# Attention in a diffusion backbone: value matmuls gathered into groups, score products between transposes, TensorE's order fixed by hand

## Chip, cores and metric

One core of a Trainium2 chip runs the whole program: two layers of a diffusion backbone over 1024 latent tokens and 256 context tokens, in fp32. The metric is the device time of one execution in microseconds (us), as the median of several runs. Lower is better.

## What is computed

Each layer normalises its input, projects it once into the inputs of four head groups, runs the groups, gates their outputs and projects back. The change concerns the two attention groups alone. Cut to what matters:

```python
def attend_dense(q, k, v):                      # latent attention: 4 heads, 1024 + 256 keys
    s = jnp.einsum('bqhd,bkhd->bhqk', q, k).astype(jnp.float32) * (q.shape[-1] ** -0.5)
    p = jax.nn.softmax(s, axis=-1).astype(v.dtype)
    return jnp.einsum('bhqk,bkhd->bqhd', p, v)
...
    def row_fn(args):                           # neighbourhood attention: a window of 8 x 16 plus 256 context keys
        ...
        s_loc = jnp.einsum('bjmhd,bijnhd->bhjmin', q_r, k_blk).astype(jnp.float32) * scale + b_r[None]
        s_ctx = jnp.einsum('bjmhd,bchd->bhjmc', q_r, kc).astype(jnp.float32) * scale
        s = jnp.concatenate([s_loc.reshape(*s_loc.shape[:4], nloc), s_ctx], axis=-1)
        p = jax.nn.softmax(s, axis=-1).astype(v.dtype)
        ...
        return (jnp.einsum('bhjmin,bijnhd->bjmhd', p_loc, v_blk)
                + jnp.einsum('bhjmc,bchd->bjmhd', p_ctx, vc))
```

In the first layer the context tokens also attend to themselves.

## The kernel before

A layer is a list of stages: projections, then latent attention, then neighbourhood attention together with the first blocks of the output projection, then the rest of the output projection. The attention stages are cut into **units**, kept in the list `units`:

- `Mla`, a *full unit*: 256 latent queries of two heads against all 1280 keys. Eight per layer, four for each pair of heads. In the first layer each pair also has a *small unit*, the 256 context queries against the context keys alone, which stands ahead of the pair's four full ones.
- `NaCtx`: the context's own queries in neighbourhood attention, two units, first layer only.
- `Na`: a block of 128 queries of two heads against 384 local and 256 context keys. Sixteen per layer: the eight of the first half of the rows (`half` 0), then the eight of the second half.

Work on a unit has four parts. `prep` makes the queries (`Mla`) or loads the bias table (`Na`). *Score products* (`scores`) write a PSUM bank of tag `psb` (five of them). VectorE takes their maximum, and ScalarE the exponential into SBUF: this is the softmax of the unit, and its row sums come with it. *Transposes* (`transpose(n)`) turn 128 x 128 pieces of the exponentials into a bank of tag `pst` (two of them), four pieces at a time, and `evac` copies the bank to a tile of tag `pt`, on ScalarE and VectorE in turn. *Value matmuls* (`values(n)`) multiply a `pt` tile by the values into the one bank `psv`. They use 64 columns of the array for each head, so the two heads write the two halves of the bank's partitions, while all other matmuls of the attention use 128 columns. An fp32 matmul runs as two instructions, a transpose as one. At the end `normalise` divides by the row sums, through two or four more transposes of line L716.

The loop at the end of `layer` goes through the units. While unit u runs its `steps`, the *pieces* of unit u+1 (its score products) are written between them, and `units[u+2].prep()` behind step `PREP` = 2. In `Mla.steps`, step k is the transposes of key block k+1 and then the value matmuls of block k, so transposes run one block ahead of values. There are ten key blocks in a full unit; a piece is the whole score work of one head and one half of the queries (three products and the softmax), and four pieces go behind steps 0, 2, 4 and 6 (`PIECES`). In `Na` the three steps are: transposes 0 and 1; values 0 and transposes 2; values 1 and 2. Its one piece is all the scores of the next unit.

This written order is not the order of the program. The kernel is built with a scheduler (`TileContext(nc, schedule_with_timeline_sim=True)`) that places each engine's instructions by its own estimate of when they are ready, within the dependencies of the tiles and their buffers, so on every engine it may pull work forward. Behind each of the last eight `Na` units the loop also writes one block of the output projection, `out_block(fb, [k0])`: 24 matmuls of 512 columns over the first 512 tokens, whose inputs (`merged(0)`) are ready when the first half has been normalised. The scheduler can use these as filler.

## Time and profile before

| | |
|---|---|
| median of 3 runs | 1508.65 us (1508.60 to 1509.43) |
| profiled execution, span from first to last instruction | 1511.4 us |
| TensorE busy in it | 1464.8 us, 97% |
| VectorE, ScalarE, GpSimd busy | 51%, 38%, 31% |
| latent attention, first and second layer | about 466 to 642 and 1165 to 1335 us from the span's start |
| neighbourhood attention, first and second layer | about 642 to 743 and 1335 to 1440 us |

The profile shows one execution, 2.7 us longer than the median of the runs. PE is TensorE, PEld its weight loads (they overlap the matmuls), DVE is VectorE, ACT ScalarE, POOL GpSimd, SP the engine that issues most DMAs. The end of a matmul in the profile is modelled, and matmuls overlap in the pipeline, so a busy PE can still lose time: the distance from one start to the next tells what a matmul costs. PEclk is the share of TensorE's full clock (2.4 GHz) that was granted; 0.50 is the lower level, 1.2 GHz.

### The profile page before, as it was taken

Reading aid. Unit: us, or ns where it says so; the run is one execution under the profiler, and the core shown is the slowest. Engines: PE = TensorE matmul, PEld = TensorE weight load, DVE = VectorE, ACT = ScalarE, POOL = GpSimd, SP = SyncE. Lnnn points to the kernel's source line nnn. Section 1 sums busy time; section 2 is a strip of 40 time slices with the busy share of each in tenths; the row PEclk is TensorE's granted clock in tenths of the full one; section 3 lists DMA queues with packets and bytes.
Section 4 is the critical chain, followed back from the end, with each engine's and each line's share of the span. In section 5 each row is a group of like instructions: output and inputs, shape, how many; then the busy total and the mean of one; then the engine's idle time right before and its main releaser. Section 6 shows DMA issues by size and latency. Waiting matters only on the chain.

```text
span 1511.4 us, 23233 instructions
## 1 busy us (share of the span) xinstructions
PE 1464.8 (97%) x8964; PEld 1176.5 (78%) x8964; DVE 772.2 (51%) x1873; ACT 575.9 (38%) x1303; POOL 464.8 (31%) x369
## 2 busy tenths in 40 slices
PE   4999999999999999999999999999999999999996
PEld 3788888988887667677788988898887776667786
DVE  5878657063026767654465752201213676754373
ACT  5511111122226656554343421112223666654442
POOL 2235334041220110535623253412231010253741
PEclk8999999999999999999999999999999999999998
DMA  9412335355450222654433101123472041663241
GB/s 355 171 58 98 112 100 169 102 178 181 140 105 1 57 57 85 129 155 116 147 123 123 42 28 43 48 89 121 155 255 38 15 83 37 155 159 98 77 149 56
DMA packets 80943, 166.46 MB, mean 110 GB/s; under 512 B 8129, under 2 KB 34753, under 8 KB 80705
## 3 DMA queue, kind: packets, MB, share of 16 engines
q1 hardware_dynamic: 63808, 136.66, 27.1%
q0 software_dynamic: 15936, 27.27, 8.9%
q8 instruction: 70, 1.15, 0.3%
q10 hardware_dynamic: 1088, 1.05, 0.2%
q14 instruction: 41, 0.33, 0.1%
HBM read 135.33 MB, written 33.82 MB: 112 GB/s over the span
## 4 chain that ended last, share of the span: by engine, by line
PE 86%; DVE 5%; POOL 3%; issue 3%; DMA 2%; ACT 1%; SPq 0%; DVEq 0%; POOLq 0%; ACTq 0%
PE psb L159 63%; PE psv L832 6%; PE pst L822 6%; PE psv L957 3%; PE pst L944 3%; PE psb L917 1%; PE psb L924 1%; POOL s L184 1%; DVE s L186 1%; DVE g L466 1%; PE pst L716 1%; POOL g L1064 1%; POOL wl L323 1%; DMA wr<-in_wtb 0%; PE pst L270 0%
## 5 line engine op out<-in xcount | busy, mean ns | idle before, releaser
L159 PE MATMUL psb<-g,wh 128*128 128x512 f32 (+1 forms) x2400 | 695.0, 374 | 0.9 <-ACT g L374 0.8
L159 PEld LDWEIGHTS psb<-g,wh 128*128 128x128 f32 x2400 | 433.4, 190 | 84.6 <-issue 2.6
L159 PE MATMUL psb<-g,wl 128*128 128x512 f32 (+1 forms) x1200 | 446.4, 373 | 0.4 <-DVE wl L323 0.4
L159 PEld LDWEIGHTS psb<-g,wl 128*128 128x128 f32 x1200 | 227.4, 189 | 42.1 <-issue 2.2
L323 POOL TENSOR_TENSOR wl<-wr,wh 128x1024 fp32r<-128x1024 f32 (+2 forms) x64 | 150.1, 2348 | 304.6 <-ACT wh L318 303.8
L701 DVE COPY pt<-pst 128x512 f32<-128x512 f32 x132 | 86.7, 657 | 119.4 <-PE pst L822 51.3
L159 PE MATMUL psb<-g,st 128*128 128x512 f32 (+1 forms) x600 | 143.0, 371 | 3.5 <-ACT wl L811 2.2
L799 DVE TENSOR_REDUCE s<-psb 128x1 f32<-128x512 f32 (+1 forms) x200 | 113.8, 588 | 39.7 <-PE psb L159 39.3
L318 ACT CAST wh<-wr 128x1024 fp32r<-128x1024 f32 (+2 forms) x56 | 56.1, 1007 | 161.6 <-PE psb L159 126.7
L159 PEld LDWEIGHTS psb<-g,st 128*128 128x128 f32 x600 | 95.6, 191 | 18.3 <-ACT wl L811 2.8
L703 ACT COPY pt<-pst 128x512 f32<-128x512 f32 (+1 forms) x132 | 73.7, 558 | 92.9 <-PE pst L822 45.6
L832 PE MATMUL psv<-pt,g 128*64 128x256 f32 x656 | 101.7, 401 | 0.4 <-DVE x L722 0.4
L298 DVE CUSTOM_DVE_ANT_0 tmp<-g,x 128x512 f32<-128x512 f32 x112 | 92.9, 882 | 10.0 <-POOL x L431 7.2
L184 POOL TENSOR_TENSOR s<-s,mhalf 128x4 f32<-128x4 f32 (+3 forms) x35 | 36.7, 1048 | 146.9 <-DVE s L240 56.2
L159 PE MATMUL psb<-g,g 128*128 128x256 f32 (+1 forms) x576 | 76.8, 289 | 0.0
L159 PEld LDWEIGHTS psb<-g,g 128*128 128x128 f32 x576 | 71.7, 191 | 0.8
L320 POOL TENSOR_SCALAR wh<-wr 128x1024 fp32r<-128x1024 f32 x16 | 44.3, 2772 | 78.1 <-PE psb L159 40.5
L159 PE MATMUL psb<-st,g 128*128 128x288 f32 (+1 forms) x456 | 64.3, 289 | 0.0
L832 PEld LDWEIGHTS psv<-pt,g 128*64 128x64 f32 x656 | 34.6, 135 | 37.2 <-issue 20.4
L811 ACT ACTIVATE g<-psb,s,rq 128x512 f32<-128x512 f32 x64 | 49.3, 776 | 34.2 <-DVE s L806 31.7
L822 PEld LDWEIGHTS pst<-ident,g 128*128 128x128 f32 x256 | 26.7, 140 | 45.1 <-issue 43.5
L159 PEld LDWEIGHTS psb<-st,g 128*128 128x128 f32 x456 | 60.4, 188 | 0.5 <-issue 0.2
(205 smaller groups left out, 2074.8 us busy)
## 6 DMA issues: line engine op xcount, KB each, us to landing
g<-in_wmod SPq DMA_DIRECT2D x48, 512.0 KB, 4.7
wr<-in_wtb SPq DMA_DIRECT2D x46, 512.0 KB, 3.8
wr<-in_wout SPq DMA_DIRECT2D x27, 512.0 KB, 4.3
st<-in_nab SPq DMA_DIRECT2D x24, 384.0 KB, 3.3
x<-in_xT SPq DMA_DIRECT2D x32, 256.0 KB, 4.4
g<-scr_q POOLq DMA_DIRECT2D x32, 256.0 KB, 5.1
x<-x SPq DMA_DIRECT2D x24, 256.0 KB, 3.1
g<-scr_k POOLq DMA_DIRECT2D x20, 256.0 KB, 4.5
```

What stands on the lines that cost most here:

```text
L159: m = pe.matmul(out, l_, r_, start=(i == 0), stop=(i == n - 1))
L184: pool.tensor_tensor(r0, v, mhalf[:, :n], ALU.pow)
L298: dve.tensor_tensor_reduce(junk, w[:, hf * 512:hf * 512 + 512], crow[cond, hf], 1.0, 0.0, ALU.mult, ALU.add, part[:, i, cond, hf:hf + 1])
L318: act.copy(hi, raw)
L323: (pool if lo_eng == "pool" else dve).tensor_tensor(lo, raw, f(hi), ALU.subtract)
L701: dve.tensor_copy(dst, src)
L703: act.copy(dst, src)
L799: dve.reduce_max(mx[:, i:i + 1], s_, AX.X)
L811: act.activation(dst, sps[i], AF.Exp, bias=nb[:, 1:2], scale=rq[:, 0, tq:tq + 1], accum_out=self.rs[:, t, h, i:i + 1])
L822: pe.transpose(pt_[:, h, t * 128:(t + 1) * 128], self.P[h, t, kk], ident)
L832: pe.matmul(self.pv[h * 64:h * 64 + 64, :], V[kk][:, hh * 64:hh * 64 + 64], self.pts[n][:, h, :], start=(n == 0), stop=(n == len(self.ks) ...
L944: pe.transpose(pt_[:, k, :], src, ident)
```

## The change

The value matmuls of a full `Mla` unit run in two groups, each behind the five transposes that it needs: T0 to T4, values 0 to 4, T5 to T9, values 5 to 9. `Na` units make three transposes each, and the values of two neighbouring units run as one group of twenty behind the second one's transposes. For this `pt` has six tiles instead of three (and the scratch space of the DMA descriptors is cut to 8192 bytes a partition). The pieces are single score products now, twelve for a full unit and three for an `Na` unit, and the loop writes one ahead of each step (a second one ahead of the first step, where the next unit has more pieces than this one has steps: `LEAD`). `normalise` is a step of its own in `Mla`. Last, all TensorE instructions of the loop are chained: `Pe.chain(True)` adds a dependency without a semaphore from each matmul to the next, so TensorE's order is the written one, and the scheduler can move nothing forward on it. The other engines are still ordered by the scheduler. The projections ahead of the loop and the code behind it are as before. (Comments were also removed; lines shift.)

```diff
-PIECES = (0, 2, 4, 6)
 PREP = 2
+LEAD = 2
...
-    pe, act, dve, pool, sp = nc.tensor, nc.scalar, nc.vector, nc.gpsimd, nc.sync
+    act, dve, pool, sp = nc.scalar, nc.vector, nc.gpsimd, nc.sync
...
-    BUFS = {"x": 20, "g": 24, "wr": 2, "wh": 2, "wl": 2, "st": 2, "tmp": 6, "pt": 3, "v1": 3, "pc": 5, "s": 12}
+    BUFS = {"x": 20, "g": 24, "wr": 2, "wh": 2, "wl": 2, "st": 2, "tmp": 6, "pt": 6, "v1": 3, "pc": 5, "s": 12}
...
+    class Pe:
+        chained, last = False, None
+        def _next(self, m):
+            if self.chained:
+                after(m, self.last)
+                self.last = m
+            return m
...
+        def chain(self, on):
+            self.chained, self.last = on, None
+    pe = Pe()
...
             def pieces(self):
-                return [lambda i=i: self.scores(i // 2, i % 2) for i in range(4)]
+                return [fn for i in range(4) for fn in self.scores(i // 2, i % 2)]
             def steps(self):
...
+                out, n = [], len(self.ks)
+                runs = [(0, n // 2), (n // 2, n)] if n > 2 else [(0, n)]
+                for a_, b_ in runs:
+                    out += [lambda k=k: self.transpose(k) for k in range(a_, b_)]
+                    out.append(lambda a_=a_, b_=b_: [self.values(k) for k in range(a_, b_)])
+                out.append(lambda: normalise(self.rs, 2, map_(2 + self.pair, self.cidx)[:, self.o:self.o + 256],
+                                             self.pv, 256))
+                return out
...
             def steps(self):
...
+                out = [lambda n=n: self.transpose(n) for n in range(3)]
+                if self.cb % 2:
+                    mate = na_units[na_units.index(self) - 1]
+                    out.append(lambda: [un.values(n) for un in (mate, self) for n in range(3)])
+                return out
...
+        pe.chain(True)
         for u, un in enumerate(units):
             for fn in before.get(u, []):
                 fn()
             steps = un.steps()
             todo = units[u + 1].pieces() if u + 1 < len(units) else []
-            n = len(steps)
+            lead = LEAD if len(todo) > len(steps) else 1
             for k, step in enumerate(steps):
+                while todo and lead > 0:
+                    todo.pop(0)()
+                    lead -= 1
+                lead += 1
                 step()
-                if todo and (n < 4 or k in PIECES):
-                    todo.pop(0)()
-                if k == min(PREP, n - 1) and u + 2 < len(units):
+                if k == min(PREP, len(steps) - 1) and u + 2 < len(units):
                     units[u + 2].prep()
             while todo:
                 todo.pop(0)()
             for fn in behind.get(u, []):
                 fn()
+        pe.chain(False)
...
-    nc = bacc.Bacc("TRN2", target_bir_lowering=False, num_devices=1)
+    nc = bacc.Bacc("TRN2", target_bir_lowering=False, num_devices=1, dynamic_dma_scratch_size=8192)
```

In the listings of the two programs a row is one instruction or several equal ones, out<-in, partitions x columns of the output. TensorE in a full unit of latent attention, before (L832 value matmuls, L822 transposes, L159 score products):

```order
L832 MATMUL psv_5083<-pt_5157,g_4191 64x256 x2
L822 MATMUL pst_5180<-ident_66,g_4852 128x128
L822 MATMUL pst_5180<-ident_66,g_4894 128x128
L822 MATMUL pst_5180<-ident_66,wl_4990 128x128
L822 MATMUL pst_5180<-ident_66,wh_5032 128x128
L159 MATMUL psb_5335<-g_4930,st_5139 128x512 x3
L159 MATMUL psb_5340<-g_4899,st_5139 128x256 x3
L832 MATMUL psv_5083<-pt_5176,g_4208 64x256 x2
```

The same place with the change (L160 is every matmul, L163 every transpose):

```order
L160 MATMUL psb_5454<-g_4888,st_5295 128x512 x3
L163 MATMUL pst_5459<-ident_66,g_5257 128x128
L163 MATMUL pst_5459<-ident_66,g_5324 128x128
L163 MATMUL pst_5459<-ident_66,wl_5348 128x128
L163 MATMUL pst_5459<-ident_66,wh_5372 128x128
L160 MATMUL psb_5466<-g_4861,st_5295 128x256 x3
L160 MATMUL psv_5479<-pt_5388,g_4225 64x256 x2
L160 MATMUL psv_5479<-pt_5400,g_4225 64x256 x2
L160 MATMUL psv_5479<-pt_5420,g_4191 64x256 x2
L160 MATMUL psv_5479<-pt_5452,g_4191 64x256 x2
L160 MATMUL psv_5479<-pt_5464,g_4191 64x256 x2
```

The value matmuls of five key blocks now follow each other; before they stood alone or in twos between the transposes. Over the whole program the listing has 238 such runs of value matmuls before and 52 with the change (two for each of the 16 full units, one for each of the 16 pairs of `Na` units and for each of the four small units of either kind).

TensorE in the first half of neighbourhood attention, before (L924 context products, L957 values, L944 transposes):

```order
L924 MATMUL psb_6559<-g_5595,g_6291 128x256 x2
L924 MATMUL psb_6559<-g_5595,g_6294 128x256 x2
L957 MATMUL psv_6336<-pt_6357,g_5831 64x128 x2
L957 MATMUL psv_6336<-pt_6357,g_5833 64x128 x2
L944 MATMUL pst_6394<-ident_66,pc_6314 128x128
L944 MATMUL pst_6394<-ident_66,pc_6315 128x128
L957 MATMUL psv_6336<-pt_6364,g_5835 64x128 x2
L957 MATMUL psv_6336<-pt_6364,g_5598 64x128 x2
L944 MATMUL pst_6407<-ident_66,g_6367 128x128 x4
```

And with the change, from the last score product of a unit (`psb_6433`, whose exponentials go to `g_6408`) to that unit's first transposes:

```order
L160 MATMUL psb_6433<-g_5595,g_5824 128x256 x2
L160 MATMUL psb_6433<-g_5595,g_5827 128x256 x2
L163 MATMUL pst_6445<-ident_66,pc_6343 128x128
L163 MATMUL pst_6445<-ident_66,pc_6344 128x128
L160 MATMUL psb_6458<-g_6285,g_6291 128x384 x2
L163 MATMUL pst_6462<-ident_66,g_6408 128x128 x4
```

Before, the transposes that need the product `psb_6559` stand 58 rows behind it in the listing; with the change two transposes and one score product stand between. Behind a unit with an odd number the group of twenty value matmuls stands there as well, and in the second half of the units a block of the output projection.

ScalarE there (exponentials of the local scores into `g`, of the context scores into `pc`), before:

```order
L933 ACTIVATE g_6548,s_6297<-g_6548,s_6565 128x384 x2
L934 ACTIVATE pc_6481,s_6297<-psb_6490,s_6496 128x256
L703 COPY pt_6452<-pst_6449 128x256
L934 ACTIVATE pc_6549,s_6297<-psb_6559,s_6565 128x256
L933 ACTIVATE g_6609,s_6297<-g_6609,s_6626 128x384 x2
```

and with the change:

```order
L970 ACTIVATE g_6408,s_5830<-g_6408,s_6439 128x384
L971 ACTIVATE pc_6409,s_5830<-psb_6433,s_6439 128x256
L970 ACTIVATE g_6408,s_5830<-g_6408,s_6439 128x384
L971 ACTIVATE pc_6410,s_5830<-psb_6433,s_6439 128x256
L724 COPY pt_6478<-pst_6473 128x512
```

Both local exponentials came first before; now one of the context stands between them, and the first transposes need both local ones.

## Rows read from the trace of the kernel before

**Rows 1.** The page's first part: busy time, share of the span, instructions.
```profile
PE 1464.8 (97%) x8964; PEld 1176.5 (78%) x8964; DVE 772.2 (51%) x1873; ACT 575.9 (38%) x1303; POOL 464.8 (31%) x369
```

**Rows 2.** Busy time by stage: stretch, its length, each engine, granted clock, DMA share, GB/s.
```profile
466.00:642.00 176.00, 172.80 (x1122) 117.03 (x1120) 120.56 (x297) 104.75 (x274) 31.84 (x41) 0.99 0.31 70
642.00:743.00 101.00, 99.47 (x710) 75.67 (x708) 53.35 (x132) 49.61 (x153) 53.95 (x38) 1.00 0.48 138
1165.00:1335.00 170.00, 168.95 (x1100) 116.38 (x1098) 116.99 (x287) 108.46 (x280) 20.18 (x27) 1.00 0.31 74
1335.00:1440.00 105.00, 103.91 (x752) 77.81 (x750) 51.53 (x124) 50.22 (x143) 64.32 (x45) 1.00 0.44 117
```

**Rows 3.** Timeline of TensorE in a full unit: start, length, line, tiles, count.
```profile
574.26 0.65 PE L832 MATMUL psv<-pt,g 128*64 128x256 f32 x4
574.84 0.44 PE L822 MATMUL pst<-ident,g 128*128 128x128 f32 x2
575.12 0.27 PE L822 MATMUL pst<-ident,wl 128*128 128x128 f32 x1
575.22 0.27 PE L822 MATMUL pst<-ident,wh 128*128 128x128 f32 x1
575.43 0.65 PE L832 MATMUL psv<-pt,g 128*64 128x256 f32 x4
...
578.79 1.08 PE L832 MATMUL psv<-pt,g 128*64 128x256 f32 x8
579.81 0.44 PE L822 MATMUL pst<-ident,g 128*128 128x128 f32 x2
```

**Rows 4.** Timeline of TensorE at the ends of two full units that follow each other.
```profile
1218.98 0.44 PE L716 MATMUL pst<-ident,tmp 128*128 128x128 f32 x2
...
1239.21 0.38 PE L716 MATMUL pst<-ident,tmp 128*128 128x128 f32 x2
```

**Rows 5.** Timeline of one softmax in a full unit, from product to last exponential.
```profile
565.63 0.60 PE L159 MATMUL psb<-g,st 128*128 128x256 f32 x3
...
566.27 0.42 DVE L799 TENSOR_REDUCE s<-psb 128x1 f32<-128x256 f32 x1 [0.56 <-PE psb L159]
...
567.11 0.78 ACT L811 ACTIVATE g<-psb,s,rq 128x512 f32<-128x512 f32 x1
...
568.64 0.56 ACT L811 ACTIVATE pc<-psb,s,rq 128x256 f32<-128x256 f32 x1
```

**Rows 6.** VectorE's and ScalarE's groups, 1335 to 1375 us: busy, mean ns, idle before.
```profile
L701 DVE COPY pt<-pst 128x512 f32<-128x512 f32 x9 | 6.2, 689 | 7.6 <-PE pst L944 5.8 <-ACT pc L934 1.7
L929 DVE TENSOR_REDUCE s<-psb 128x2 f32<-128x512 f32 x6 | 4.1, 681 | 0.6 <-PE psb L924 0.6
L701 DVE COPY pt<-pst 128x256 f32<-128x256 f32 x4 | 1.7, 424 | 6.2 <-PE pst L944 6.2
...
L931 DVE TENSOR_REDUCE s<-s 128x2 f32<-128x4 f32 x5 | 0.7, 148 | 0.0
...
L934 ACT ACTIVATE pc<-psb,s 128x256 f32<-128x256 f32 x15 | 7.1, 472 | 6.2 <-PE pst L944 6.2
L933 ACT ACTIVATE g<-g,s 128x384 f32<-128x384 f32 x10 | 6.1, 613 | 1.7 <-DVE s L931 1.7
```

**Rows 7.** Timeline of TensorE in neighbourhood attention: products, then values, then transposes.
```profile
653.21 0.96 PE L917 MATMUL psb<-g,g 128*128 128x384 f32 x4
654.00 0.64 PE L924 MATMUL psb<-g,g 128*128 128x256 f32 x4
654.57 0.66 PE L957 MATMUL psv<-pt,g 128*64 128x128 f32 x8
655.16 0.44 PE L944 MATMUL pst<-ident,pc 128*128 128x128 f32 x2
```

**Rows 8.** A long wait of TensorE, and busy time and clock just behind it.
```profile
470.72 2.05 PE L159 MATMUL psb<-g,st 128*128 128x256 f32 x6 [2.21 <-ACT wl L811]
...
471.93:475.34 3.41, 3.41 (x13) 2.71 (x12) 1.74 (x5) 2.22 (x7) 0.00 (x0) 0.50 0.00 0
```

More of the change, by code (lines that the diff above doesn't have):

```diff
@@ L793, in scores, with product @@
                 qs = slice(t * 128, t * 128 + 128)
[L794 to L796 removed]
+                st = {}
+                def product(i):
+                    c = keys[i]
+                    if i == 0:
+                        st["mx"], st["sps"] = T("s", [len(keys)]), []
                     s_ = PS("b", [CHUNKS[c][1]])
                     mm3(s_, [(Q[:, 0, h, qs], Q[:, 1, h, qs], K[h, c][:, 0, :], K[h, c][:, 1, :])])
[L799 to L800 removed]
@@ L817, in transpose @@
+                return [lambda i=i: product(i) for i in range(len(keys))]
             def transpose(self, n):
@@ L903, in scores, with local @@
                 half, pair, cb = self.half, self.pair, self.cb
-                g = self.group()
-                qd, rs = g["qd"], g["rs"]
                 qs = slice(cb * 128, cb * 128 + 128)
-                mx = T("s", [2, 2])
-                pl = self.pl = T("g", [2, 384])
-                pc = self.pc = [T("pc", [256]) for _ in range(2)]
-                bt = self.bt
-                for h in range(2):
+                st = {}
+                def local(h):
+                    qd = self.group()["qd"]
+                    if h == 0:
+                        st["mx"] = T("s", [2, 2])
+                        self.pl = T("g", [2, 384])
+                        self.pc = [T("pc", [256]) for _ in range(2)]
                     hh = 2 * pair + h
@@ new lines, in context @@
+                def context():
+                    g = self.group()
+                    qd, rs, mx, pl, pc = g["qd"], g["rs"], st["mx"], self.pl, self.pc
+                    s_ = PS("b", [2, 256])
+                    prev = None
+                    for h in range(2):
+                        for hl in range(2):
+                            m = pe.matmul(s_[:, h, :], qd[h][:, hl, qs], kc_[0][:, 2 * pair + h, :],
+                                          start=(hl == 0), stop=(hl == 1))
+                            if hl == 0:
+                                after(m, prev)
+                            prev = m
+                    dve.reduce_max(mx[:, :, 1:2], s_, AX.X)
+                    nb = T("s", [2, 1])
+                    dve.reduce_max(nb, mx, AX.X, negate=True)
+                    for h in range(2):
+                        act.activation(pl[:, h, :], pl[:, h, :], AF.Exp, bias=nb[:, h, :], accum_out=rs[:, cb, h, 0:1])
+                        act.activation(pc[h], s_[:, h, :], AF.Exp, bias=nb[:, h, :], accum_out=rs[:, cb, h, 1:2])
@@ L936, in layer @@
+                return [lambda: local(0), lambda: local(1), context]
             jobs = [[(i, h) for i in range(5) for h in range(2)][b0:b0 + 4] for b0 in (0, 4, 8)]
```

85 lines of the change are left out of this document (28 added, 57 removed).

## Prediction

> **What bounds the kernel now.** I read the busy times first. TensorE is busy for 97% of the span, every other engine for about half or less [rows 1]. By stage it is the same in both attentions: 172.8 of 176 us, 99.5 of 101, 169.0 of 170 and 103.9 of 105 [rows 2]. So nothing keeps TensorE waiting there for more than 6.9 us in all (552 less 545.1), and a gain has to come out of time in which TensorE counts as busy.
>
> That time shows in the timeline, where I compare starts [rows 3]. A group of value matmuls for one key block (four instructions) starts at 574.26 and the transposes behind it at 574.84: 0.58 us. A group for two blocks takes 579.81 - 578.79 = 1.02 us. So a block costs 0.44, and 0.14 comes once per group. The four transposes between two groups take 575.43 - 574.84 = 0.59 us; transposes that follow each other stand 0.10 to 0.11 apart (575.12 to 575.22), so four should take 0.44, and 0.15 is lost around the group as well. In all a **group of value matmuls costs 0.29 us, whatever its size**; I use 0.30. It is lost where TensorE goes from 128 columns to 64 and back.
>
> A rule of the Trainium skill speaks against reading it so. "TensorE: Matmul & The Clock Gate", in Part 3 under "The mechanism", says that a weight load overlaps running matmuls only where it is for other rows of the array. All value matmuls use the same 128 rows, so by that each one would pay its own load and a longer group would save nothing; eight instructions would take 1.16 us. The row says 1.02, so the measurement decides against it, but it is a rival below.
>
> **What the change removes.** The listing has 238 groups before and 52 now: 186 x 0.30 = **55.8 us less**. The transposes, products and values themselves stay as many. The six `pt` tiles and the smaller descriptor space cost no instruction; GpSimd, which writes descriptors, is busy for 31% [rows 1], so I cost them at nothing. If everything else ran as before, that would be the result. Since TensorE's order is now the written one, the 6.9 us of waits before also go, and new ones come. I add those up.
>
> **Neighbourhood attention, units without filler.** Before, the scheduler had pulled score products about two units ahead. Now the last product of a unit (context) stands just ahead of the last transposes of the unit in front, and its first transposes need its softmax. One round, from a unit's first transposes to the next one's: transposes 0.44, one product 0.40 (half of 654.00 - 653.21), transposes 0.44, context product 0.64 to the end of its row [rows 7]: 1.92. Then the maximum 0.68, the small maximum 0.15, and local, context and local exponential 0.61 + 0.47 + 0.61 [rows 6]: 4.44. Four hand-overs of about 0.05 (566.23 to 566.27 in a softmax [rows 5]) make 4.64. On VectorE a copy of transposes stands in the way, in every second unit the 0.42 of the third one ahead of the small maximum, in the others part of a 0.69 ahead of the large one [rows 6]; I take 0.3. So **4.95 us a unit**. TensorE's work in it is 0.40 + 0.40 + 0.48 of products, ten transposes 1.1, values 1.1 (five halves of 0.44, which is 655.16 - 654.57 less 0.15) and half a group 0.15: 3.62 [rows 3, 7]. In even units it stands idle for about 2.6 us; in odd ones the twenty value matmuls (2.4 us) fill the time. The mean wait is 1.33; with eight such units a layer, 16 x 1.33 = 21, and 1 for the division, whose VectorE work falls into the same chain: **22 us more**. Behind the later eight units a block of 24 matmuls of 0.23 us hides the chain, so they keep the gain.
>
> **Latent attention, full units.** Here ten transposes and twelve products alternate. The last product is followed by five blocks of values (5 x 0.44 + 0.30), two transposes 0.22 and one product 0.70 before the next unit's first transposes: 3.4 us of cover. Its softmax takes from 566.23 to 569.20, 2.97 us [rows 5], and 0.2 for the pipeline and the hand-over, 3.2. So it just fits where VectorE and ScalarE are free. Written out with both queues in their new order, the exponentials of the product group before are still running when the last ones could start, which makes T0 late by some 0.5 us. The bounds are 0 and 2.1 (a whole group of three exponentials in front, 567.11 to 569.20). I take 0.5, the end that the working is nearest to: 14 units x 0.5 = **7 us**.
>
> **Places with little to fill.** Behind each small unit seven products follow each other, and then transposes that need the last of them: the nearest row is the wait of 2.21 us that such a place had before [rows 8]. With five banks and a softmax of three exponentials in 2.1 us I get 4 for each, **8 us** for two. The last unit of each layer's latent attention, and the one ahead of the second small unit, have only two to four products; about 20 of their transposes follow each other with two banks, each pair held by 0.69 of copying, 0.25 more each: **5 us**. The keys of the second head pair and the entries into the next stage have no row; between 0 and the 2.21 of rows 8 for four places I take 1 each, **4 us**.
>
> **The clock.** Behind the wait that ended at 470.72 the granted clock was 0.50 for 3.41 us [rows 8], the level of 1.2 GHz, so up to 1.7 us of work was lost. The idle 2.6 us of eight even units (four a layer) are as long. Over these stages nothing else fell (0.99 to 1.00 [rows 2]). I take two of the eight: **3 us**, and keep 0 and 14 for the range.
>
> **Sum.** -55.8 - 6.9 + 22 + 7 + 8 + 5 + 4 + 3 = -13.7 us against the profiled execution's 1511.4, thus 1497.7. That execution is 2.7 us longer than the median; I take the difference off the median: 1508.65 - 13.7 = **1495 us**.
>
> **Rivals.**
> 1. *The new waits are half of it.* The schedulers of VectorE and ScalarE may put the softmax first and keep the chain below 4.4. For it speaks that ScalarE is busy for half of these stages only. Half of 49 us of waits is 24.5 less: about 1471.
> 2. *The clock falls behind every idle even unit, and behind the two small units.* Each costs up to 1.7: 10 x 1.7 = 17 instead of 3, and the chain of 4.95 grows with it: about 1509, no change. Against it: only a wait of 2.2 shows it here, none below 1.2.
> 3. *Slower: the last softmax of a full unit is not covered.* The place is T0 of each of the 14 units. Cover and need differ by 0.2 us, so each us that VectorE or ScalarE comes late lands in the time, 14 times. From 0.5 + 13.7 / 14 = 1.5 us a unit it cancels the gain; at the bound of 2.1 the time is 1495 + 14 x 1.6 = 1517. For it: VectorE has some 15 us of work in a unit that lasts 20.2 now [rows 4] and would last 18.5. Against it: before, with the same work on both engines, no such wait shows, though TensorE had more to choose from.
> 4. *Grouping saves nothing*, the page's rule above. Then the 55.8 stay and the waits come: 1495 + 56 = 1551. The 1.02 of rows 3 speaks against it.
>
> **How the numbers follow.** My case (1485 to 1503) has 0.47, the first rival 0.22, the second 0.14, the third 0.14, the fourth 0.03. The likeliest gives 1495. The range reaches over the first rival down to 1468 and up to 1514, over the second and most of the third; beyond are the fourth, the worst of the third and an almost free change, together under 0.2. A measurement can tell about 0.2%, 3 us, from no change. Faster than 1505.6: my case, the first rival and a third of the second, 0.74. Within 3 us: most of the rest of the second and a little of the third, 0.11. Slower: 0.15.
>
> **What would show it.** Right: groups of value matmuls of 20 instructions 2.3 to 2.5 us long, and 0.3 us around each; about 18.4 us from one division to the next in latent attention, where it was 20.2 [rows 4]; in the first eight units of neighbourhood attention waits of transposes for ScalarE of 2 to 3 us every second unit, and none in the last eight. Busy TensorE falls by some 50 us or more while idle time grows. Wrong: attention stages no shorter although the groups are there (waits on ScalarE at T0 of every full unit), a granted clock well below 1 in them, or value matmuls that are still spaced by their loads.

## The result, and the profile after

The changed kernel took 1522.39 us (median of 7, 1511.88 to 1524.41) against 1508.68 us before on the same chip: a ratio of 1.0075, with a 95% interval of 1.0053 to 1.0097. It is slower by 14 us between the medians (11 by the ratio, as the seven times of the change are spread), where 1495 us was forecast, 14 less. On another chip the same program came to 1.0032 (1.0018 to 1.0047). Its profiled execution spans 1519.2 us.

The page's first part, answering to [rows 1]:

```profile
PE 1434.4 (94%) x8964; PEld 1205.3 (79%) x8964; DVE 778.4 (51%) x1873; ACT 580.1 (38%) x1303; POOL 460.5 (30%) x369
```

TensorE runs as many instructions as before and is busy for 30 us less. So the groups did save time, and more than that was given back as idle time. To see where, I compare stretches that begin and end at the same instruction in both programs (TensorE's order outside the loop is unchanged). The attention of the first and the second layer, in the view of busy time by stretch, before:

```profile
454.42:780.13 325.71, 320.79 (x2127) 232.66 (x2125) 196.25 (x470) 174.27 (x468) 98.69 (x89) 0.99 0.37 98
1168.55:1440.16 271.61, 270.25 (x1839) 192.35 (x1837) 165.98 (x402) 155.98 (x417) 84.50 (x71) 1.00 0.36 92
```

and after, whole and then by stage (latent attention, first and second half of neighbourhood attention, of the first layer and of the second; the 8.3 us of the context's own queries, at 637, are left out):

```profile
453.78:793.76 339.98, 307.52 (x2127) 248.31 (x2126) 203.39 (x477) 178.99 (x472) 99.25 (x89) 0.96 0.35 93
1181.71:1450.75 269.04, 251.81 (x1839) 203.46 (x1838) 168.60 (x402) 157.90 (x417) 83.75 (x69) 0.99 0.37 92
...
453.78:637.19 183.41, 166.87 (x1131) 129.16 (x1129) 119.96 (x285) 108.55 (x274) 21.37 (x27) 0.96 0.20 49
645.45:688.32 42.87, 34.03 (x311) 29.49 (x311) 24.34 (x70) 24.48 (x79) 13.92 (x17) 0.92 0.67 156
688.32:793.76 105.44, 99.84 (x637) 84.52 (x636) 52.27 (x102) 42.12 (x108) 56.37 (x36) 0.98 0.45 138
1181.71:1336.09 154.38, 149.18 (x1051) 115.59 (x1049) 108.92 (x254) 100.50 (x252) 20.02 (x25) 1.00 0.30 68
1336.09:1378.25 42.16, 33.53 (x313) 29.36 (x311) 24.29 (x70) 23.01 (x73) 17.04 (x19) 0.92 0.52 126
1378.25:1450.75 72.50, 69.10 (x480) 58.51 (x479) 35.39 (x78) 34.39 (x93) 46.69 (x26) 1.00 0.42 123
```

The attention takes 609.0 us where it took 597.3: 14.3 more in the first layer, 2.6 less in the second. TensorE is idle for 49.7 us of it (609.02 less 559.33) where it was for 6.3, and the granted clock is down to 0.92 in two stages that had 1.00.

The scheduler before had moved instructions across the borders of stages, so stage lengths don't compare directly. What does is the **time lost**: the length of a stage less its own instructions, each at its usual distance from start to start in the trace of before (a 512-column product 232 ns, 384 columns 180, 256 columns 119, a transpose 109, a pair of value matmuls 215 or 107). It holds the cost of the groups, the waits and the low clock. The forecast column is the prediction's own terms, put to their stages.

| time lost, us | before | forecast | after | of it low clock |
|---|---|---|---|---|
| latent attention, first layer | 28.0 | 25.9 | 34.1 | 7.3 |
| context's own queries | 1.3 | 0.8 | 2.2 | 0 |
| neighbourhood, first half, first layer | 8.1 | 14.2 | 15.4 | 3.4 |
| neighbourhood, second half, first layer | 10.0 | 2.6 | 10.0 | 2.1 |
| latent attention, second layer | 21.8 | 13.4 | 15.7 | 0 |
| neighbourhood, first half, second layer | 7.8 | 14.1 | 14.7 | 3.4 |
| neighbourhood, second half, second layer | 9.4 | 2.2 | 6.1 | 0 |
| sum | 86.4 | 73.2 | 98.2 | 16.2 |

The low-clock column is length times what the granted clock lacks to 1.00; before it came to 1.8 in all. It is rough, as the granted clock is read to two places: the nine stretches at 0.50 that this profile has in the attention, 3.41 us each, lost 1.7 us of work apiece, 15.4 together. Of the 25 us that the forecast misses, 8 lie in the first layer's latent attention and 11 in the two second halves of neighbourhood attention. The two first halves, where the waits were expected, miss by 2.

The groups themselves look as forecast. Timeline of TensorE, a full unit's last product, its second group and the division behind it:

```profile
490.10 0.62 PE L160 MATMUL psb<-g,st 128*128 128x256 f32 x3 [0.37 <-ACT wl L841]
490.65 2.38 PE L160 MATMUL psv<-pt,g 128*64 128x256 f32 x20
492.96 0.44 PE L163 MATMUL pst<-ident,tmp 128*128 128x128 f32 x2
```

The twenty instructions of a group (five key blocks of four) take 2.31 us, to the start of the division's transposes. From one division to the next a full unit of the second layer takes 18.63 us, where it took 20.2 [rows 4]:

```profile
1208.77 0.44 PE L163 MATMUL pst<-ident,tmp 128*128 128x128 f32 x2
...
1227.40 0.44 PE L163 MATMUL pst<-ident,tmp 128*128 128x128 f32 x2
```

Now the new waits. In an even unit of neighbourhood attention, first half (timeline; the rows are TensorE, VectorE and ScalarE in order of time):

```profile
657.63 0.60 PE L163 MATMUL pst<-ident,g 128*128 128x128 f32 x4
...
658.78 0.72 PE L160 MATMUL psb<-g,g 128*128 128x256 f32 x4
...
659.11 0.69 DVE L722 COPY pt<-pst 128x512 f32<-128x512 f32 x1
...
659.71 0.68 DVE L966 TENSOR_REDUCE s<-psb 128x2 f32<-128x512 f32 x1
...
660.62 0.61 ACT L970 ACTIVATE g<-g,s 128x384 f32<-128x384 f32 x1 [0.43 <-DVE s L968]
...
661.38 0.33 PE L163 MATMUL pst<-ident,g 128*128 128x128 f32 x1 [1.30 <-ACT g L970]
...
661.68 0.60 ACT L970 ACTIVATE g<-g,s 128x384 f32<-128x384 f32 x1
...
662.43 0.47 PE L163 MATMUL pst<-ident,g 128*128 128x128 f32 x2 [0.72 <-ACT g L970]
```

The context product at 658.78 is the next unit's last. Its maximum waits for a copy of transposes, then come the exponentials, and the second head's transposes start at 662.43: 4.80 us from the unit's first transposes to these, 4.95 forecast.

At the small unit of latent attention (timeline of TensorE):

```profile
468.39 4.56 PE L160 MATMUL psb<-g,st 128*128 128x256 f32 x15 [2.25 <-ACT g L841]
472.79 0.49 PE L163 MATMUL pst<-ident,pc 128*128 128x128 f32 x3
475.60 0.33 PE L163 MATMUL pst<-ident,pc 128*128 128x128 f32 x1 [2.33 <-ACT pc L841]
```

The products of the next full unit follow each other until the banks run out (2.25), and its first transposes then wait for the last exponential (2.33). The same happens at the second small unit, with 2.25 and 2.76.

At the end of the first layer's neighbourhood attention (timeline of VectorE, and the last row TensorE's):

```profile
754.88 0.68 DVE L722 COPY pt<-pst 128x512 f32<-128x512 f32 x1
755.48 2.11 DVE L735 COPY tmp<-s 128x512 f32<-128x512 f32 x1
757.51 2.29 DVE L344 TENSOR_TENSOR wl<-wr,wh 128x1024 fp32r<-128x1024 f32 x1
759.72 1.75 DVE L245 TENSOR_TENSOR tmp<-tmp,tmp 128x512 f32<-128x512 f32 x1
761.38 0.41 DVE L722 COPY pt<-pst 128x256 f32<-128x256 f32 x1
...
761.85 0.70 PE L160 MATMUL psv<-pt,g 128*64 128x128 f32 x4 [3.68 <-DVE pt L722]
```

The last four value matmuls wait 3.68 us for a copy of 0.41, which VectorE's queue holds behind 6 us of other work: the copy for the division (L735), a split of weights for the projection (L344) and a sum of squares (L245). All three are slow here, which the last section takes up. TensorE had a whole block of that projection left to do, but the chain keeps it behind the group.

Last, the clock (busy time by stretch; the figure behind POOL's is the granted clock):

```profile
468.14:471.56 3.42, 3.17 (x9) 2.65 (x10) 1.44 (x4) 2.78 (x9) 0.00 (x0) 0.50 0.00 0
467.00:474.00 7.00, 4.89 (x18) 3.90 (x18) 3.81 (x11) 4.97 (x13) 0.00 (x0) 0.76 0.00 0
...
661.00:667.00 6.00, 4.90 (x36) 4.28 (x38) 2.84 (x11) 2.79 (x10) 4.66 (x5) 0.72 0.35 120
671.00:677.00 6.00, 3.46 (x31) 2.74 (x30) 3.90 (x12) 3.17 (x10) 1.30 (x2) 1.00 0.02 4
```

Behind the wait at 661 the clock fell to its lower level for a while; behind the next even unit's, which is no shorter, it did not. In this execution it fell behind four of the eight even units, behind three of the four long waits at the small units (twice in a row behind the last) and behind the 3.68.

### The profile page after: what moved, and what is told of

Its sections match the earlier page's. It is cut to its first block, busy times and chain, and to the rows that moved or that the text cites. A ratio compares the mean times of both kernels' runs of the same rounds, so it can differ in the third digit from the quotient of the medians.

```text
span 1519.2 us, 23106 instructions
## 1 busy us (share of the span) xinstructions
PE 1434.4 (94%) x8964; PEld 1205.3 (79%) x8964; DVE 778.4 (51%) x1873; ACT 580.1 (38%) x1303; POOL 460.5 (30%) x369
## 4 chain that ended last, share of the span: by engine, by line
PE 81%; DVE 10%; ACT 4%; issue 3%; POOL 1%; DMA 0%; SPq 0%; DVEq 0%; ACTq 0%; POOLq 0%
PE psb L160 67%; PE pst L163 7%; PE psv L160 6%; PE pst L160 2%; DVE pt L722 1%; DVE s L824 1%; ACT g L970 1%; POOL s L205 1%; DVE g L951 1%; ACT wl L841 1%; DVE s L207 1%; DVE g L487 1%; DVE tmp L735 1%; POOL wl L344 1%; ACT g L841 1%
## 5 line engine op out<-in xcount | busy, mean ns | idle before, releaser
L160 PE MATMUL psb<-g,wh 128*128 128x512 f32 (+1 forms) x2400 | 690.3, 373 | 0.2 <-DVE g L396 0.2
L160 PEld LDWEIGHTS psb<-g,wh 128*128 128x128 f32 x2400 | 433.6, 190 | 85.4 <-issue 2.3
L160 PE MATMUL psb<-g,wl 128*128 128x512 f32 (+1 forms) x1200 | 445.2, 371 | 0.0
L160 PEld LDWEIGHTS psb<-g,wl 128*128 128x128 f32 x1200 | 227.2, 189 | 41.8 <-issue 1.0
L344 POOL TENSOR_TENSOR wl<-wr,wh 128x1024 fp32r<-128x1024 f32 (+2 forms) x64 | 150.8, 2359 | 305.8 <-ACT wh L339 304.7
L160 PE MATMUL psb<-g,st 128*128 128x512 f32 (+1 forms) x616 | 164.8, 383 | 11.4 <-ACT g L841 5.9
L824 DVE TENSOR_REDUCE s<-psb 128x1 f32<-128x512 f32 (+1 forms) x200 | 117.5, 592 | 70.3 <-PE psb L160 67.4
L160 PE MATMUL psb<-g,g 128*128 128x256 f32 (+2 forms) x832 | 140.4, 310 | 1.4 <-ACT g L841 1.4
L160 PE MATMUL psv<-pt,g 128*64 128x256 f32 (+1 forms) x1312 | 121.4, 335 | 5.5 <-DVE pt L722 5.2
L160 PEld LDWEIGHTS psb<-g,st 128*128 128x128 f32 x616 | 98.7, 195 | 30.9 <-ACT g L841 9.0
L160 PEld LDWEIGHTS psb<-g,g 128*128 128x128 f32 x832 | 112.5, 197 | 4.9 <-ACT g L841 2.3
L160 PEld LDWEIGHTS psv<-pt,g 128*64 128x64 f32 x1312 | 80.7, 139 | 34.5 <-DVE pt L722 6.6
L163 PE MATMUL pst<-ident,g 128*128 128x128 f32 x464 | 86.6, 280 | 20.9 <-ACT g L970 17.5
L163 PEld LDWEIGHTS pst<-ident,g 128*128 128x128 f32 x464 | 60.1, 142 | 42.4 <-ACT g L970 21.9
L1127 DVE SCALAR_TENSOR_TENSOR x<-psb,modG,x 128x512 f32<-128x512 f32 (+1 forms) x48 | 29.6, 616 | 101.3 <-PE psb L160 80.6
L341 POOL TENSOR_SCALAR wh<-wr 128x1024 fp32r<-128x1024 f32 x16 | 44.5, 2783 | 117.4 <-PE pst L163 62.9
L160 PE MATMUL psb<-st,g 128*128 128x288 f32 (+1 forms) x456 | 64.3, 289 | 0.0
```

What stands on the lines that cost most here:

```text
L160: return self._next(nc.tensor.matmul(*p, **k))
L163: return self._next(nc.tensor.transpose(*p, **k))
L341: pool.tensor_scalar(hi, raw, 1.0, None, ALU.mult)
L344: (pool if lo_eng == "pool" else dve).tensor_tensor(lo, raw, f(hi), ALU.subtract)
L824: dve.reduce_max(st["mx"][:, i:i + 1], s_, AX.X)
L1127: dve.scalar_tensor_tensor(xa, p, mod[l]["G"][:, fb, cond:cond + 1], xa, ALU.mult, ALU.add)
```

## The experiments

Theory A: a group costs about 0.30 us wherever it stands, so the grouping gives back its 55 us, and the fixed order loses more than that at a few named places, where too little independent work was written in front of a softmax or a copy. The rivals B stand in the expectations. Each run's "before" is the kernel before on the same chip.

**1. No chain.** `pe.chain(True)` becomes `pe.chain(False)`.

> The changed kernel, but TensorE's instructions of the attention loop are not chained, so the scheduler may move them. In its listing the 52 groups of value matmuls fall apart into 205. Theory A (a group costs 0.30 us wherever it stands; the written order's waits and the clock drops behind them give the gain back): no waits to speak of, and 33 groups fewer than before, so 10 us less than before: 1499, between 1496 and 1504. Rival B (groups are worth much less than 0.30 us, because their cost hides in waits anyway): the same as before, 1508 or more.

Measured 1495.95 us, ratio 0.9909 (0.9894 to 0.9923). TensorE is idle for 5.8 us of the attention (588.6 us), and the time lost is 77.6 us, 8.8 less than before: 0.27 for each of the 33 groups, or 0.21 without the low-clock stretch of [rows 8] (1.7 us), which this profile lacks. So the chain keeps the groups together, and the chain brings the waits.

**2. Products two units ahead in the first half of neighbourhood attention.**

```diff
-LOADS = (..., (0, "k2 k3 q1"), (3, "v3"), (5, "q2"), (9, "q3"))
+LOADS = (..., (-1, "k2 k3 q1"), (2, "v3"), (4, "q2"), (9, "q3"))
-    BUFS = {..., "s": 12}
+    BUFS = {..., "s": 16}
...
+        def ahead(u):
+            return 3 if n0 <= u < n0 + 7 else 0
...
-            todo = units[u + 1].pieces() if u + 1 < len(units) else []
...
+            todo = take(u + 1, 99) + take(u + 2, ahead(u))
...
+                want = -(-m * (k + 1) // n) if u >= n0 else min(m, lead + k)
```

Here `take(i, n)` hands out the next n products of unit i, and `want` spreads the products of a unit evenly over the steps of the unit in front, in both halves of neighbourhood attention.

> The changed kernel, but in the first eight units of neighbourhood attention the score products are written two units ahead instead of one (loads of keys and queries moved to match). Theory A: the 27 us that these stages lose beyond their instructions and groups (20 of waits, 7 at the low clock, both layers together) fall to 5 or less, the granted clock there is 1.00: 1500, between 1495 and 1505. Rival B (the chain of maximum and exponentials is bound by VectorE and ScalarE with their copies, however early the products stand): transposes still wait for ScalarE in even units, above 1515.

Measured 1486.97 us, 0.9841 (0.9821 to 0.9860). That is more than expected, but 14 us of it lie outside the attention (run 6). Its fair control is run 6 at 0.9945: the difference is 16 us, where 22 was expected. The first layer's stage shows it best:

```profile
634.89:666.77 31.88, 30.56 (x311) 26.73 (x311) 23.81 (x70) 24.33 (x82) 10.41 (x12) 1.00 0.53 146
...
1308.94:1345.27 36.33, 32.21 (x312) 28.23 (x311) 23.78 (x70) 22.90 (x76) 15.90 (x18) 0.95 0.59 141
```

The same 311 matmuls take 31.88 us instead of 42.87, VectorE and ScalarE are as busy as before in the shorter time, and the clock is back at 1.00. The waits for ScalarE's exponentials there come to 0.9 us, where they were 8.8. Rival B falls: neither engine was the bound. In the second layer 36.33 remain of 42.16, with one wait of 2.81 us for a copy on VectorE, and VectorE had itself stood idle for the load of a bias table (timeline of VectorE):

```profile
1322.81 0.56 DVE L951 CUSTOM_DVE_ANT_0 g<-psb,st 128x384 f32<-128x384 f32 x1 [5.38 <-DMA st<-in_nab]
```

The change has no wait of VectorE for such a load, so it came with the earlier products. It is there in runs 8 and 12 as well, with 3.50 and 3.72 us.

**3. The output block ahead of the group of twenty.**

```diff
+                if True and k == len(steps) - 1 and u in outs and un.cb % 2:
+                    outs.pop(u)()
                 step()
```

> The changed kernel, but in the second half of neighbourhood attention the block of the output projection behind an odd unit is written ahead of the group of twenty value matmuls, not behind it. Theory A: the two waits of value matmuls for a copy on VectorE (3.7 us in the first layer, 1.5 in the second) go, as 5.6 us of matmuls stand in front, and so does the clock drop behind the first: 5 to 8 us less, 1515 to 1518. Rival B (the copy stands behind whatever VectorE's order puts in front, and gets later with the matmuls): no change, 1522.

Measured 1507.72 us, 0.9982 (0.9972 to 0.9992), below the expected range. Against the change's first result that is 14.7 us less, against its control (run 5, at 1.0032) 0.5%, or 7.5 us. By the traces the attention takes 5.8 us less than in the change's first profile, as expected, and the time lost in the two second halves falls from 10.0 and 6.1 to 3.6 and 3.3 us. The last group now starts with its copies done, all forty instructions in one piece (timeline of TensorE):

```profile
759.25 2.40 PE L160 MATMUL psv<-pt,g 128*64 128x128 f32 x40
```

**4. The small units behind the first full unit.**

```diff
-            if not last:
-                units.append(Mla(pair, 1024, 2, (2,)))
             for qb in range(4):
                 units.append(Mla(pair, qb * 256, qb // 2, (0, 1, 2)))
+                if not last and qb == 0:
+                    units.append(Mla(pair, 1024, 2, (2,)))
...
+            return 9 if u + 2 < nm and len(units[u + 1].keys) == 1 else 0
...
+            todo = take(u + 1, 99) + take(u + 2, ahead(u))
```

> The changed kernel, but in the first layer's latent attention the small unit of each pair stands behind the pair's first full unit, and 9 of the 12 products of the full unit behind it are written during that first full unit (eight tiles for the context's exponentials instead of five). Theory A: the 16 us that are lost around the two small units (11 of waits, 5 at the low clock) fall to 3 or less: 1509, between 1505 and 1513. Rival B (the loss belongs to the small units wherever they stand, since their softmaxes are as long): 1518 or more.

Measured 1511.81 us, 1.0019 (1.0003 to 1.0035), inside the range. But it is half a hit. The first layer's latent attention loses 27.5 us instead of 34.1; the clock is 1.00 there, which alone was 7.3, while 13.8 of the 16.5 idle us remain. So what the stage gained is no more than the low clock. The long waits for exponentials went, and 5.0 us of waits for the division's operand took their place (0.8 in the change):

```profile
483.93 0.41 PE L163 MATMUL pst<-ident,tmp 128*128 128x128 f32 x2 [1.41 <-DVE tmp L735]
```

**5. The change again**, as control.

> The changed kernel itself once more, on the chip of the three below, as their control: about 1520, with low-clock stretches behind the same waits but not in every execution (1512 to 1524 in its first seven). If the first 100 us take 2 us less here than in its first profile, as in the runs of the last call, that part belongs to the chip and not to the kernels.

Measured 1515.47 us (1510.87 to 1519.25), 1.0032. Its profiled execution loses 9.0 us to the clock instead of 16.2, with the same waits, and its attention takes 603.7 us instead of 609.0. The first stretches take 2 us less here too, so that part is not the kernels'.

**6. Sixteen small tiles alone.** `"s": 12` becomes 16.

> The changed kernel with 16 small tiles (tag s) instead of 12 and nothing else; the run with the products two units ahead had them too, and was 14 us faster outside the attention stages. If the small tiles did that: 14 us less than the control, and the two stretches of projections ahead of the attentions take 382 us each where they take 390 and 388. If the loads that moved did it: no change, and then that run's 14 us are not explained.

Measured 1501.24 us, 0.9945 (0.9925 to 0.9965): 14.2 less than the control. The stretches ahead of the attentions take 382.1 and 382.3 us.

**7. Values of each block alone again, order still fixed.**

```diff
+                out.append(lambda: self.transpose(0))
+                for k in range(n - 1):
+                    out.append(lambda k=k: (self.transpose(k + 1), self.values(k)))
+                out.append(lambda: self.values(n - 1))
...
+                return [lambda: (self.transpose(0), self.transpose(1)),
+                        lambda: (self.values(0), self.transpose(2)),
+                        lambda: (self.values(1), self.values(2))]
```

> The changed kernel with its fixed order and its single products, but with the values of each key block behind the next block's transposes as before the change: 227 groups instead of 52. Theory A (0.30 us for a group, on top of the waits): 175 x 0.30 = 52 more than the control, less the part that falls into waits of the first eight neighbourhood units (some 10): 40 to 55 more, 1560 to 1575. Rival B (the cost of a group is a modelling error of mine, and the fixed order alone costs the time): within 10 of the control.

Measured 1582.49 us, 1.0478 (1.0461 to 1.0495): 67 more than the control, above the range. A full unit of the second layer takes 22.90 us instead of 18.63 for ten groups instead of two (timeline of TensorE):

```profile
1316.99 0.65 PE L160 MATMUL psv<-pt,g 128*64 128x256 f32 x4
1317.57 0.63 PE L160 MATMUL psb<-g,st 128*128 128x256 f32 x3
1318.04 0.38 PE L163 MATMUL pst<-ident,g 128*128 128x128 f32 x2
...
1327.94 0.62 PE L160 MATMUL psb<-g,st 128*128 128x256 f32 x3
1329.97 0.41 PE L163 MATMUL pst<-ident,tmp 128*128 128x128 f32 x2 [1.41 <-DVE tmp L735]
```

The four instructions of a group take 0.58 as in [rows 3], 0.15 more than their usual 0.43. The three products behind them take 0.47 instead of 0.36 (3 x 119 ns), and 0.09 is lost ahead of the group: 0.35 in all, where it was 0.30 between transposes. Eight groups make 2.8 of the 4.3 us. The rest is a wait that I had not expected: the division now comes one product after the last small group, and its transposes wait for VectorE. So the grouping is worth what was forecast, and the groups of ten had also covered the division. Rival B falls.

**8. The three repairs together** (runs 2, 3 and 4, with the products ahead from the unit before neighbourhood attention on).

> All three repairs together and 16 small tiles: products two units ahead from the last latent unit to the eighth neighbourhood unit, output blocks ahead of the value groups, small units behind the pair's first full unit with 9 products written early. Theory A: the attention stages take 597 - 55 and some 15 of remaining waits (0.5 in each full unit and the bare transposes), about 557 where the change has 609; with 14 less outside, 1455, between 1448 and 1465, and the granted clock of the attention stages is 0.99 or 1.00. Rival B (repairs get into each other's way, as all three crowd VectorE and ScalarE): 1470 or more.

Measured 1476.65 us, 0.9777 (0.9762 to 0.9791), 22 us above the forecast. The attention takes 578.6 us where 557 was expected. By their own traces the three repairs had saved 16.1, 5.8 and 9.5 of 609.0, which makes 577.6. That it fits so well is partly the clock's doing, which fell nine times in the change's profile, five, seven and four times in those of runs 2, 3 and 4, and twice in this one. Without that (1.7 us each) the time lost is 9, 6 and -1 us less in the three runs than in the change, and 20 less in this one. Either way the repairs do not get into each other's way, and rival B falls too, though the time is in its range. What was wrong was my 15 us for the waits that remain elsewhere.

**9. Sixteen small tiles in the kernel before.**

> The kernel before with 16 small tiles instead of 12, nothing of the change. If the small tiles act ahead of the attentions whatever order those have: 14 us less than before, 1496. If they act only with the written order: no change. It tells how much of the 33 us that the run with all three repairs gained belongs to the attention.

Measured 1494.91 us, 0.9905 (0.9887 to 0.9923), as by the first case. So of the 2.2% of run 8 about 1.0% has nothing to do with the attention.

**10. The chain on latent attention alone.** `if u == nm: pe.chain(False)` in the loop.

> The changed kernel with TensorE's chain ended where latent attention ends, so that the scheduler orders neighbourhood attention (117 groups in the listing). Theory A (the written order pays in the full latent units and loses in neighbourhood attention): latent attention takes the change's time, neighbourhood attention that of the run without a chain, which lies 15 to 17 us lower: about 1499, between 1494 and 1504. Rival B (what neighbourhood attention loses is handed on to the stages behind it when it goes): 1510 or more.

Measured 1503.73 us, 0.9957 (0.9945 to 0.9969), at the upper end. Neighbourhood attention takes the times of run 1 (35.9 and 100.5 us in the first layer in both runs), but the place where the chain ends costs a new wait of 2.1 us in the first layer, and latent attention of the second grows from 154.4 to 160.3 us: 4 of it are instructions of the next stage that moved in, 2 are lost. The change loses in neighbourhood attention. In latent attention it gains in the second layer (15.7 us lost where it was 21.8), but loses around the small units of the first (34.1 where it was 28.0), and this run, chained there alone, is some 7 us slower than run 1 without any chain (0.9957 to 0.9909).

**11. The division behind the next unit's first transposes.** In each latent and context unit `normalise` is put off until then; also the third product of an odd neighbourhood unit is written ahead of its group of twenty.

> The run with all three repairs, and in addition each latent or context unit's division is written behind the first transposes of the next unit (its transposes waited 1.57, 1.24, 0.90 and 1.44 us for VectorE, the first two twice), and the third product of an odd neighbourhood unit stands between its last transposes and its group of twenty (a wait of 2.87 us there in the second layer). Theory A (waits at named places add up): some 8 us less than the run with all three, 1468, between 1464 and 1473. Rival B (the waits move to the next copy on VectorE): 1475 or more.

Measured 1499.74 us, 0.9930 (0.9913 to 0.9948): 23 us *more* than run 8. The second layer shows why (timeline; what is written late also comes late on VectorE):

```profile
1190.17 0.41 DVE L824 TENSOR_REDUCE s<-psb 128x1 f32<-128x256 f32 x1
...
1190.88 0.16 DVE L730 TENSOR_REDUCE s<-s 128x4 f32<-128x12 f32 x1
...
1191.08 0.18 DVE L732 RECIPROCAL s<-s 128x4 f32<-128x4 f32 x1
1191.29 0.29 DVE L735 COPY tmp<-s 128x256 f32<-128x256 f32 x1
...
1191.73 0.41 PE L163 MATMUL pst<-ident,tmp 128*128 128x128 f32 x2 [1.57 <-DVE tmp L735]
```

The sums, reciprocals and their copy moved with the transposes that need them, behind the maximum of a product that stands after them in the text. Every full unit, which had no such wait, now loses some 1.7 us.

**12. VectorE's part early, the transposes where they were.** `normalise` is cut in two, and the sums, reciprocals and copy are written ahead of the unit's last group; they need the row sums alone.

> The run with all three repairs, and in addition VectorE's part of each division (sums, reciprocals and their copy, which need the row sums alone) is written ahead of the unit's last group of value matmuls; the transposes of the division stay behind that group, where they stood, and the third product of an odd neighbourhood unit stands ahead of its group of twenty. Theory A (transposes wait for whatever VectorE's queue was given too late): the waits of 1.57, 1.24, 0.90, 1.44 and 2.87 us go, 1468 (1464 to 1473), where writing the whole division later added 1.7 us to every latent unit. Rival B (VectorE's copies of transposes come later instead and hold the value matmuls): 1475 or more.

Measured 1472.39 us, 0.9751 (0.9738 to 0.9765), the fastest of all and at the upper end of the range, with half the gain that theory A put on it. By TensorE's idle time, which is 0.16 to 0.22 us shorter than the expectation's figures for the same waits, those of 1.41 and 1.07 at the small units are gone, though one of 1.21 for the next unit's queries stands there now. Those of 0.72 and 1.26 at the context's own queries stay, and what was 2.65 and 0.48 in the second layer is 1.92 and 1.22. The 2.65 was no matter of VectorE's order: VectorE waits for its bias table there (run 2). The attention takes 574.2 us, 4.4 less than in run 8, of which 1.7 are one more low-clock stretch in run 8's profile. Against run 9, which has the same small tiles and none of the change, it is about 1.5% faster.

## Why the prediction was wrong

**Groups: 55.8 us less, 0.30 each.** Held: 0.21 to 0.27 by run 1, 0.35 by run 7, where products stand next to the groups. With the twenty instructions of a group in 2.31 us, no run bears out the rule of the Trainium skill by which grouping would save nothing ("TensorE: Matmul & The Clock Gate", Part 3, "The mechanism"), the fourth rival.

**Neighbourhood units without filler: 22 us more.** Held, mechanism and size: 4.80 us for the chain, time lost 15.4 and 14.7 where 14.2 and 14.1 were forecast, and the first layer's went when the products were written earlier (run 2). The first rival, by which the new waits would be half of it, did not occur.

**Full latent units: 0.5 each.** The size came out, 18.63 us where 18.4 was forecast, but by luck: T0, the place of the forecast, does not wait. A product does, for a bank that an exponential still reads, 3.7 us over the second layer's seven full units behind the first, 0.53 each.

**"Behind the later eight units a block of 24 matmuls of 0.23 us hides the chain, so they keep the gain."** This step failed, by 11 us. The block does hide the softmax. But the group of twenty needs copies on VectorE, and the block was written *behind* the group, so nothing covers a late copy: 3.68 us in the first layer, 1.5 in the second, with a clock drop behind the first. Run 3 shows it: with the block in front the two halves lose 3.6 and 3.3 us instead of 10.0 and 6.1. How late the copy comes is in part a matter of slow instructions in front of it (last section). I had followed only one of the two things that the order made TensorE wait for.

**Places with little to fill: 8 us at the small units.** Undersized. From 463 to 477 and from 555 to 570 us, around the two small units, 7.1 and 8.8 us are lost: 11 without the low clock, which takes the other 5 and of which the forecast had put nothing there. Latent attention of the first layer misses by 8. The waits of 2.3 to 2.8 us are as in [rows 8], but there are two at each place. I had also counted the 6.9 us of waits of before as gone, while their largest, the 2.21 of [rows 8], is still there as 2.25. The 5 us for bare transposes were not far off: waits of transposes for copies come to 3.3 us in the two latent attentions. The 4 us for entries were not measured apart.

**The clock: 3 us, "two of the eight".** Undersized, 16.2 us in this execution and 9.0 in the second profile, against 1.8 before. This is the second rival in part: the clock fell behind four of eight even units, not all, and in nine stretches altogether, where the rival had ten and the sum two. By itself it moves the sum by 16.2 - 1.8 - 3 = 11 us, to 1506. It was not independent of the waits: in one profile each, the first half of neighbourhood attention of run 2's first layer and the latent attention of run 4 had 1.00 once their waits were gone or shorter.

The three failing terms make the 25 us (11 at the second halves, 8 in the first layer's latent attention, the rest in small amounts over the other four stages; the clock's part is inside these). The third rival, T0 of the full units, did not occur; the 15 us of VectorE's work in a unit that it rests on are 13.9 by [rows 2] (116.99 of 170.00, in 20.2). That the sign turned is due to terms that I had put at nothing or too small, all of them waits at single places and the low clock behind them.

## What to carry to other kernels

Fixing an engine's order by hand takes from the scheduler the right to fill a wait, so every wait in the written order has to be covered by hand: go through each place where the fixed engine needs another engine's result, copies of operands too, and write independent work in front of it, not behind. A saving that comes from grouping is kept only if the products that feed the next softmax are written early enough; here the same groups were 0.3 to 0.8% slower than before, or 2.5% faster (1.0% of that from elsewhere). What another engine has to deliver should be written when its inputs are there, apart from the instruction that uses it (run 12 against run 11).

## What was not expected of the hardware

**Small tiles made matmuls faster.** Four more tiles of 160 bytes a partition took 14 and 15 us off the two programs. The waits explain little of it: with them one wait of 2.0 us and the low clock behind it went from the first layer's projections, 3.7 us in all. The rest is spread evenly. The same instructions, projections ahead of the first attention, before and in run 9 (busy time by stretch of each):

```profile
64.14:454.42 390.28, 388.06 (x2248) 338.06 (x2247) 193.48 (x551) 82.09 (x143) 126.17 (x93) 1.00 0.39 126
```

```profile
60.86:442.98 382.12, 381.91 (x2249) 337.46 (x2247) 193.62 (x551) 81.98 (x143) 126.54 (x93) 1.00 0.40 129
```

The median distance between 512-column products is 232 ns in the first and 227 in the second, over the 2227 of them ahead of both layers' attention, which makes 11 us. On every engine both programs run the same instructions in the same order. By the text of the programs only the room for four tiles differs, and so, in all likelihood, where the tiles behind them lie in SBUF. No trace shows the addresses, so that is argued, and what it is about the place stays open.

**The clock is not the same from one execution to the next.** The same program and the same waits lost 16.2 us in one profile and 9.0 in another, and the changed kernel's executions spread over 12.5 us, where the four of the kernel without a chain lie within 2.4.

**Three instructions of VectorE took far longer beside GpSimd.** The copy that held TensorE for 3.68 us stood behind L735, L344 and L245, which took 2.11, 2.29 and 1.75 us. The copy of L735 elsewhere, and what GpSimd does beside the first two (timeline of VectorE and of GpSimd):

```profile
666.94 0.43 DVE L735 COPY tmp<-s 128x512 f32<-128x512 f32 x1
...
754.95 2.35 POOL L344 TENSOR_TENSOR wl<-wr,wh 128x1024 fp32r<-128x1024 f32 x1
757.27 3.65 POOL L1097 TENSOR_TENSOR g<-x,g 128x512 fp32r<-128x512 f32 x2
```

The eight copies of this kind take 0.43 us in the four places where GpSimd is idle, and 1.16 (twice) and 2.11 (twice) beside its L344 and L1097. L344 and L245 take 1.22 and 0.69 us where GpSimd is idle. At those lengths the three would be done at 757.8 and the late copy at 758.2, just when TensorE began to wait for it, so by this estimate the wait was as much one of slow instructions as of a long queue. Beside other work of GpSimd L245 keeps its length (0.68 at 709.81, beside L341 and L344), and no run took GpSimd's work away, so that GpSimd is the cause is not shown. Run 3 covers the wait either way.
